# A mean over rows on one core: the first two megabytes in eight loads of sixteen partitions, and another way to fill the selector

## The chip, the cores and the metric

The kernel runs on one core of one Trainium2 chip. The metric is the device time of one execution in microseconds (us). Before the change the median of three runs is 1243.44 us (1243.44 to 1243.58).

## The reference, cut to what matters

```python
def setup_inputs():
    return {"x": np.random.randn(64, 256, 8192).astype(np.float32)}

def reference(x):
    return np.mean(x, axis=2)
```

16384 rows of 8192 float32 numbers are averaged, each to one number: 536.87 MB are read and 65.5 KB written, with about one addition for every four bytes read.

## The kernel before, in words

**Who owns which rows.** A row is 32 KB. SBUF has 128 partitions, and each partition p owns 127 rows that lie side by side in memory (`owned`, line 39), so that what partition p reads begins 127 rows, some 4.16 MB, behind what partition p-1 reads. That leaves the last 128 rows. They are cut into quarters, and each quarter row is summed in a partition of its own (`groups`, line 40).

**The loads.** There are three buffers of 128 x 16384 numbers, 8 MB each (line 53), each for a pair of rows per partition. SyncE (SP) issues every load, in one queue, in the order in which the code has them (lines 109 to 137):

- Line 114 loads the first FIRST = 2048 columns of the first pair, 1 MB over all 128 partitions, and tells `first_sem`. Line 115 loads the other 14336 columns, 7 MB, and tells `in_sems[0]`.
- Line 117 loads the second and third pair, 8 MB each.
- The loop of lines 118 to 123 waits until a buffer is free and loads the next pair into it, 60 times.
- Lines 125 to 131 load the 127th row of every partition (4 MB), three groups of quarter rows (1 MB each) and the fourth group in four pieces (448, 288, 160 and 128 KB).
- Lines 133 and 135 store the results.

**The sums.** VectorE (DVE) waits for `first_sem` (line 156). It then enters a loop that, for each buffer, waits for `in_sems[b]` and sums both rows of the pair in one reduction (line 163, 60 times), which sets the buffer free. The first reduction thus needs `first_sem` and `in_sems[0]`. The last three pairs, the single row and the quarter groups follow in straight line (lines 169 to 198), two pieces of the last group on ScalarE (ACT, lines 203 to 209).

**The selector.** A quarter group leaves one partial sum per partition, in a column of `part`; partitions 4g to 4g+3 belong to the same row g of the group. TensorE (PE) adds the four by a product with `sel`, a 128 x 32 tile that is 1/8192 where partition p belongs to row g, that is where p - 4g is 0, 1, 2 or 3, and zero elsewhere (line 218). GpSimd (POOL) makes this tile at the very start: a fill with 1/8192 (line 81) and two affine selections that put zeros on either side of the band (lines 83 and 93). PE waits for it at line 215 before anything else. POOL's next work is the scaling of the owned sums at line 104, which waits for the end.

Of the kernel before, what the change touches and what calls it, by code (L numbers as in the profile page):

```python
# [11 lines left out]
def bass_global_avg_pool_1d_kernel(  # L12
# [4 lines left out]
    P = 128  # L17
    ALIGN = 4096
    B, C, L = x.shape
    rows = B * C  # L20
    inv = 1.0 / float(L)
# [7 lines left out]
    PER = 4  # L29
    G = P // PER  # L30
# [1 line left out]
    cuts = [0, 7 * W // 16, 23 * W // 32, 7 * W // 8, W]  # L32
    pieces = [(cuts[i], cuts[i + 1]) for i in range(len(cuts) - 1)]
    NP = len(pieces)
    FIRST = L // 4

    flat = x.rearrange("b c l -> (b c) l")
    out_flat = out.rearrange("b c -> (b c)")
    owned = flat[0 : P * OWN, :].rearrange("(p r) l -> p (r l)", p=P)
# [4 lines left out]
    with ExitStack() as ctx:  # L44
# [6 lines left out]
        sel = sb("sel", [P, G])  # L51
        sb("pad", [P, (-nc.sbuf_base % ALIGN) // 4])
        bufs = [sb(f"buf{i}", [P, 2 * L]) for i in range(NBUF)]
# [6 lines left out]
        first_sem = sem("first_sem")  # L60
# [6 lines left out]
        sel_sem = sem("sel_sem")  # L67
# [10 lines left out]


        eng = nc.gpsimd  # L80
        eng.memset(sel[:], inv).then_inc(sel_sem, 1)  # L81
        eng.wait_ge(sel_sem, 1)
        eng.affine_select(  # L83
            out=sel[:],
            in_=sel[:],
            compare_op=mybir.AluOpType.is_ge,
            fill=0.0,
            base=0,
            pattern=[[-PER, G]],
            channel_multiplier=1,  # L90
        ).then_inc(sel_sem, 1)
        eng.wait_ge(sel_sem, 2)
        eng.affine_select(  # L93
            out=sel[:],
            in_=sel[:],
            compare_op=mybir.AluOpType.is_ge,
            fill=0.0,
            base=PER - 1,
            pattern=[[PER, G]],
            channel_multiplier=-1,  # L100
        ).then_inc(sel_sem, 1)
        eng.wait_ge(free_sems[0], 1)
        eng.wait_ge(owned_sem, 4)
        eng.tensor_scalar(  # L104
# [4 lines left out]
        eng = nc.sync  # L109
# [1 line left out]
        later = owned[:, 2 * NBUF * L : 2 * NB * L].rearrange(  # L111
            "p (i b w) -> b p i w", i=ROUNDS, b=NBUF
        )
        eng.dma_start(bufs[0][:, 0:FIRST], owned[:, 0:FIRST]).then_inc(first_sem, 16)
        eng.dma_start(bufs[0][:, FIRST:], owned[:, FIRST : 2 * L]).then_inc(in_sems[0], 16)
        for b in range(1, NBUF):
            eng.dma_start(bufs[b][:], pair(b)).then_inc(in_sems[b], 16)
# [23 lines left out]
        eng = nc.vector  # L141
# [11 lines left out]
                accum_out=to,  # L153
            ).then_inc(done, 1)

        eng.wait_ge(first_sem, 16)
        early = res[:, 0 : 2 * ROUNDS * NBUF].rearrange(
            "p (i b j) -> p i b j", i=ROUNDS, b=NBUF
        )
# [43 lines left out]
        eng = nc.scalar  # L203
# [8 lines left out]


        eng = nc.tensor
        eng.wait_ge(sel_sem, 3)

        def gather(dst, n, start, stop):
            return eng.matmul(dst, part[:, n : n + 1], sel[:], start=start, stop=stop)  # L218
# [41 lines left out]
```

## Time and profile before

| | |
|---|---|
| median of three runs | 1243.44 us |
| the profiled execution: its own time | 1243.53 us |
| its span, first to last instruction | 1242.3 us |
| around the span | 1.23 us |
| DVE busy | 1085.5 us, 87% of the span |
| DMA queue, packets' time | 99.8% of 16 engines' span |
| read from memory | 536.87 MB, 432 GB/s over the span |
| POOL busy, all of it | 2.1 us |
| the granted clock | 1.00 |

The span is the time from the first to the last instruction on the core. "Busy" counts an engine's own work, without its waits. The 16 DMA engines move data between memory (HBM) and SBUF in packets; a share of 99.8% says that all sixteen had a packet in hand for nearly the whole span. "SPq" and "DVEq" are the sequencers of these engines: waits, branches and the issuing of DMAs. "To landing" is the time from the issue of a DMA until its last completion.

### The profile page before, as it was taken

Reading aid. Unit: us, or ns where it says so; the run is one execution under the profiler, and the core shown is the slowest. Engines: PE = TensorE matmul, PEld = TensorE weight load, DVE = VectorE, ACT = ScalarE, POOL = GpSimd, SP = SyncE. Lnnn points to the kernel's source line nnn. Section 1 sums busy time; section 2 is a strip of 40 time slices with the busy share of each in tenths; the row PEclk is TensorE's granted clock in tenths of the full one; section 3 lists DMA queues with packets and bytes.
Section 4 is the critical chain, followed back from the end, with each engine's and each line's share of the span. In section 5 each row is a group of like instructions: output and inputs, shape, how many; then the busy total and the mean of one; then the engine's idle time right before and its main releaser. Section 6 shows DMA issues by size and latency. Waiting matters only on the chain. (4 is left out here: it accounts for less than half of the span.)

```text
span 1242.3 us, 636 instructions
## 1 busy us (share of the span) xinstructions
PE 1.7 (0%) x14; PEld 0.6 (0%) x14; DVE 1085.5 (87%) x78; ACT 3.0 (0%) x6; POOL 2.1 (0%) x8
## 2 busy tenths in 40 slices
PE   0000000000000000000000000000000000000000
PEld 0000000000000000000000000000000000000000
DVE  2898988989889898898898988989889898898988
ACT  0000000000000000000000000000000000000000
POOL 0000000000000000000000000000000000000000
DMA  9999999999999999999999999999999999999998
GB/s 405 439 439 439 439 433 411 439 439 439 439 439 422 422 439 439 439 439 439 433 411 439 439 439 439 439 437 407 439 439 439 439 439 437 409 437 439 439 439 374
DMA packets 10514, 536.94 MB, mean 432 GB/s; under 512 B 1297, under 2 KB 1554, under 8 KB 1810
## 3 DMA queue, kind: packets, MB, share of 16 engines
q1 hardware_dynamic: 10514, 536.94, 99.8%
HBM read 536.87 MB, written 0.07 MB: 432 GB/s over the span
## 5 line engine op out<-in xcount | busy, mean ns | idle before, releaser
L163 DVE TENSOR_REDUCE res<-buf 128x16384 f32 x60 | 1033.2, 17220 | 146.8 <-DVEq L162 146.8
L173 DVE TENSOR_REDUCE res<-buf 128x2 f32<-128x16384 f32 x2 | 34.4, 17220 | 4.0 <-DMA buf<-in_x_dram 4.0
L145 DVE CUSTOM_DVE_ANT_0 buf<-buf 128x4096 f32<-128x4096 f32 (+2 forms) x7 | 17.3, 2497 | 4.1 <-DMA buf<-in_x_dram 4.1
L209 ACT ACTIVATE buf<-buf 128x896 f32<-128x896 f32 (+1 forms) x2 | 1.4, 711 | 1236.7 <-DMA buf<-in_x_dram 1236.6
L104 POOL TENSOR_SCALAR scaled<-res 128x127 f32<-128x127 f32 x1 | 1.4, 1362 | 1233.3 <-DVE res L145 1233.3
L218 PE MATMUL psum<-sel,part 128*1 128x32 f32 x14 | 1.7, 225 | 1239.2 <-DVE part L145 1238.3
L209 ACT ACT_TABLE_LOAD x1 | 1.3, 1283 | 0.8 <-PEq L245 0.8
L218 PEld LDWEIGHTS psum<-sel,part 128*1 128x1 f32 x14 | 0.6, 81 | 1240.1 <-issue 1235.9
L196 DVE TENSOR_REDUCE part<-buf 128x1 f32<-128x256 f32 x1 | 0.4, 420 | 0.4 <-DMA buf<-in_x_dram 0.4
L200 DVE COPY row<-psum 1x32 f32<-1x32 f32 x1 | 0.2, 179 | 0.4 <-PE psum L218 0.4
L209 ACT ACTIVATION_READ_ACCUMULATOR buf<-buf 128x1 f32 x2 | 0.4, 188 | 0.0
L145 DVE DVE_READ_ACCUMULATOR2_ANT part<- 128x1 f32 x4 | 0.3, 82 | 0.0
L145 DVE DVE_READ_ACCUMULATOR2_ANT res<- 128x1 f32 x3 | 0.2, 83 | 0.0
L211 ACT ACTIVATE row<-psum 1x96 f32<-1x96 f32 x1 | 0.2, 223 | 0.0
L93 POOL TENSOR_SCALAR_AFFINE_SELECT sel<-sel 128x32 f32<-128x32 f32 x1 | 0.2, 215 | 0.1
L83 POOL TENSOR_SCALAR_AFFINE_SELECT sel<-sel 128x32 f32<-128x32 f32 x1 | 0.2, 213 | 0.1
L81 POOL MEMSET sel<- 128x32 f32 x1 | 0.1, 125 | 0.3 <-POOLq L245 0.3
L245 POOL MEMSET const-uint8-127<- 128x1 uint8 x1 | 0.1, 103 | 0.0
L245 POOL MEMSET const-bfloat16-1.0<- 128x1 bf16 x1 | 0.1, 102 | 0.0
L245 POOL MEMSET const-float32-0.0<- 128x1 f32 x1 | 0.1, 99 | 0.3 <-issue 0.3
L245 POOL MEMSET const-float32-1.0<- 128x1 f32 x1 | 0.1, 99 | 0.0
## 6 DMA issues: line engine op xcount, KB each, us to landing
buf<-in_x_dram SPq DMA_DIRECT2D x1, 7168.0 KB, 21.1
buf<-in_x_dram SPq DMA_DIRECT2D x4, 1024.0 KB, 34.1
buf<-in_x_dram SPq DMA_DIRECT2D x1, 4096.0 KB, 31.1
buf<-in_x_dram SPq DMA_DIRECT2D x62, 40.3
buf<-in_x_dram SPq DMA_DIRECT2D x1, 448.0 KB, 37.7
buf<-in_x_dram SPq DMA_DIRECT2D x1, 288.0 KB, 37.9
buf<-in_x_dram SPq DMA_DIRECT2D x1, 160.0 KB, 37.9
buf<-in_x_dram SPq DMA_DIRECT2D x1, 128.0 KB, 37.8
```

The costliest lines, as they stand in the source:

```text
L83: eng.affine_select(out=sel[:], in_=sel[:], compare_op=mybir.AluOpType.is_ge, fill=0.0, base=0, pattern=[[-PER, G]], channel_multiplier=1, ...
L93: eng.affine_select(out=sel[:], in_=sel[:], compare_op=mybir.AluOpType.is_ge, fill=0.0, base=PER - 1, pattern=[[PER, G]], channel_multipli ...
L104: eng.tensor_scalar(scaled[:], res[:], inv, None, op0=mybir.AluOpType.mult).then_inc(pool_sem, 1)
L145: eng.tensor_tensor_reduce(ap[:, 0:n], ap[:, 0:n], ap[:, n : 2 * n], scale=1.0, scalar=0.0, op0=ADD, op1=ADD, accum_out=to,).then_inc(done, 1)
L163: eng.tensor_reduce(early[:, bass.ds(i, 1), b, :], bufs[b][:].rearrange("p (j l) -> p j l", j=2), X, ADD,).then_inc(free_sems[b], 1)
L173: eng.tensor_reduce(res[:, 2 * g : 2 * g + 2], bufs[b][:].rearrange("p (j l) -> p j l", j=2), X, ADD,).then_inc(free_sems[0] if b == 0 els ...
L196: eng.tensor_reduce(part[:, PER + 2 : PER + 3], group(PER - 1)[:, a:z], X, ADD).then_inc(part_d, 1)
L200: eng.tensor_copy(row[:, P - G : P], psum[1][:, 0:G]).then_inc(row_sem, 1)
L209: eng.activation(ap, ap, COPY, accum_out=part[:, to : to + 1]).then_inc(part_a, 1)
L211: eng.activation(row[:, 0 : P - G], psum[0][:, 0 : P - G], COPY).then_inc(row_sem, 1)
L218: return eng.matmul(dst, part[:, n : n + 1], sel[:], start=start, stop=stop)
L245: nc = _bacc.Bacc("TRN2", target_bir_lowering=False, num_devices=1)
```

## The change

FIRST becomes 4096 columns. These first columns of the first pair, 2 MB, come in STEP = 8 loads in place of one: load j fetches 16 KB into each of the sixteen partitions j, j+8, ..., j+120, so that it has sixteen runs of 16 KB, 256 KB in all. The load behind them has the other 12288 columns, 6 MB in place of 7. DVE waits for 128 counts of `first_sem` in place of 16. The bytes that are read stay the same.

The selector is first filled with zeros, and then four affine selections, q = 0 to 3, write 1/8192 wherever p - 4g = q. Each waits for the one before it. PE waits for five counts in place of three.

```diff
-    FIRST = L // 4
+
+    FIRST = L // 2
+    STEP = 8
...
-        eng.memset(sel[:], inv).then_inc(sel_sem, 1)
-        eng.wait_ge(sel_sem, 1)
-        eng.affine_select(
-            out=sel[:],
-            in_=sel[:],
-            compare_op=mybir.AluOpType.is_ge,
-            fill=0.0,
-            base=0,
-            pattern=[[-PER, G]],
-            channel_multiplier=1,
-        ).then_inc(sel_sem, 1)
-        eng.wait_ge(sel_sem, 2)
...
+        eng.memset(sel[:], 0.0).then_inc(sel_sem, 1)
+        for q in range(PER):
+            eng.wait_ge(sel_sem, q + 1)
+            eng.affine_select(
+                out=sel[:],
+                in_=sel[:],
+                compare_op=mybir.AluOpType.not_equal,
+                fill=inv,
+                base=-q,
+                pattern=[[-PER, G]],
+                channel_multiplier=1,
+            ).then_inc(sel_sem, 1)
...
-        eng.dma_start(bufs[0][:, 0:FIRST], owned[:, 0:FIRST]).then_inc(first_sem, 16)
+        for j in range(STEP):
+            eng.dma_start(
+                bufs[0][j:P:STEP, 0:FIRST], owned[j:P:STEP, 0:FIRST]
+            ).then_inc(first_sem, 16)
...
-        eng.wait_ge(first_sem, 16)
+        eng.wait_ge(first_sem, 16 * STEP)
...
-        eng.wait_ge(sel_sem, 3)
+        eng.wait_ge(sel_sem, PER + 1)
```

More of the change, by code (lines that the diff above doesn't have):

```diff
@@ L80, in bass_global_avg_pool_1d_kernel @@
         eng = nc.gpsimd
-        eng.memset(sel[:], inv).then_inc(sel_sem, 1)
-        eng.wait_ge(sel_sem, 1)
-        eng.affine_select(
-            out=sel[:],
-            in_=sel[:],
-            compare_op=mybir.AluOpType.is_ge,
-            fill=0.0,
-            base=0,
-            pattern=[[-PER, G]],
-            channel_multiplier=1,
-        ).then_inc(sel_sem, 1)
-        eng.wait_ge(sel_sem, 2)
[L93 to L101, printed above, removed]
+        eng.memset(sel[:], 0.0).then_inc(sel_sem, 1)
[10 more added lines that the diff above has]
+            ).then_inc(sel_sem, 1)
         eng.wait_ge(free_sems[0], 1)
```

## The prediction

> **What bounds the kernel now.** I read the page first: the sliced rows, the memory line and the chain, then the loop's line.
>
> ```profile
> span 1242.3 us, 636 instructions
> ...
> DVE  2898988989889898898898988989889898898988
> ...
> DMA  9999999999999999999999999999999999999998
> ...
> HBM read 536.87 MB, written 0.07 MB: 432 GB/s over the span
> ...
> L163 DVE TENSOR_REDUCE res<-buf 128x16384 f32 x60 | 1033.2, 17220 | 146.8 <-DVEq L162 146.8
> ```
>
> The DMA row is full from the first slice to the last, DVE's is not: its 60 reductions take 17.22 us each, and 146.8 us of waiting stand before them, released by line 162, the wait for a load. So the loads are late and DVE is not. Next, busy time in stretches of time (columns: stretch, its length, then each engine, and at the end the granted clock, the DMA share and GB/s):
>
> ```profile
> 0.00:2.00 2.00, 0.00 (x0) 0.00 (x0) 0.00 (x0) 1.21 (x1) 0.74 (x7) 1.00 0.21 37
> 2.00:3.00 1.00, 0.00 (x0) 0.00 (x0) 0.00 (x0) 0.07 (x1) 0.00 (x0) 1.00 0.75 229
> 3.00:4.00 1.00, 0.00 (x0) 0.00 (x0) 0.00 (x0) 0.00 (x0) 0.00 (x0) 1.00 0.96 401
> ...
> 22.65:42.00 19.35, 0.00 (x0) 0.00 (x0) 17.24 (x2) 0.00 (x0) 0.00 (x0) 1.00 1.00 434
> ```
>
> The loads come up slowly (37, 229, 401 GB/s) and then hold 434 GB/s. Last, the start and the end in order of time:
>
> ```profile
> 0.80 0.42 SPq L114 DMA_DIRECT2D buf<-in_x_dram  x1
> 0.99 0.21 POOL L83 TENSOR_SCALAR_AFFINE_SELECT sel<-sel 128x32 f32<-128x32 f32 x1
> 1.27 0.41 SPq L115 DMA_DIRECT2D buf<-in_x_dram  x1
> 1.27 0.21 POOL L93 TENSOR_SCALAR_AFFINE_SELECT sel<-sel 128x32 f32<-128x32 f32 x1
> 1.73 1.04 SPq L117 DMA_DIRECT2D buf<-in_x_dram  x2
> 22.65 17.22 DVE L163 TENSOR_REDUCE res<-buf 128x16384 f32 x1 [22.65 <-DVEq L162]
> 40.15 19.62 SPq L121 DMA_DIRECT2D buf<-in_x_dram  x2
> ```
> ```profile
> 1239.35 0.46 DVE L145 CUSTOM_DVE_ANT_0 buf<-buf 128x288 f32<-128x288 f32 x1 [0.54 <-DMA buf<-in_x_dram]
> ...
> 1240.17 0.42 DVE L196 TENSOR_REDUCE part<-buf 128x1 f32<-128x256 f32 x1 [0.35 <-DMA buf<-in_x_dram]
> ```
>
> These add up to the span. The first packet starts at 1.8 us (the DMA view of the first 6 us is empty up to there). 536.87 MB at 434 GB/s are 1237.0 us. The last reduction starts as its load lands, at 1240.17, and 2.1 us of small work follow. 1242.3 - 2.1 - 1237.0 - 1.8 leaves 1.4 us for the slow start and the last landing. What the loads lose anywhere is lost at the end, for no later stretch has a faster rate to win it back with; what DVE, POOL or SP lose under their cover is free.
>
> **The selector.** It takes out two selections of 0.21 us and adds four of the same shape; starts lie 0.28 apart (0.99, 1.27). Four end at about 0.99 + 3 x 0.28 + 0.21 = 2.0 us, some 0.6 later than now. PE's first product comes at 1235.9 us, and POOL's next work waits for the end of the owned sums at 1234.8. That cover is 1230 us deep: 0. Without it the price would be 0.6 us.
>
> **SP's queue.** Seven more issues stand ahead of line 115's. One takes 0.42 us, and starts lie 0.47 apart (0.80, 1.27, 1.73), so 7 x 0.47 = 3.3 us: line 115 is issued at about 4.6, line 117 by 5.5. SP's next task is at 40.15. The DMA engines must not run dry meanwhile. A 256 KB load at 434 GB/s lasts 0.60 us, longer than the 0.47 of an issue, and the eight last 4.8, from 1.8 to 6.6 or later, while line 115's packets can start at 4.6 + 1.0 = 5.6 (the first load: issued at 0.80, first packet 1.8). Cover of 1.0 us: 0. If an issue took 0.65 us, it would be gone.
>
> **More completions.** Seven more loads must each report. At the tail, 288 KB land between ACT's start at 1238.67 and DVE's at 1239.35, 0.68 us, just what 434 GB/s makes of them; the next 160 and 128 KB take 0.82 instead of 0.68, so 0 to 0.07 us a load, 0 to 0.5 for seven. I take 0.2.
>
> [...]
>
> **DVE's first wait** for 128 counts ends well before line 115's load lands, which DVE awaits next: 0.
>
> **Sixteen partitions at a time.** Here is the price that decides. Every load of this trace that carries weight covers all 128 partitions, and sixteen DMA engines together hold 434 GB/s, 27.1 each. Where that ceiling sits, no row tells. If each engine has it by itself, eight loads cost nothing more. [...] 2.097 MB at 434 GB/s are 4.83 us, at 217 they are 9.66. The ends are 0 and +4.83 (coarser groupings, four engines to an entry, would give +14.5). [...] That is a judgement; the trace holds no transfer over fewer partitions at a rate that tells.
>
> [...]
>
> **Sum.** 1243.53 (the profiled execution) + 4.83 + 0.2 - 0.3 = 1248.26. The profiled execution stands 0.09 above the median: 1248.2 us. Own range of this case: 1247.1 (the whole start won) to 1248.8.
>
> **Rivals.**
>
> 1. *Full rate, not slower.* Place: the eight loads. If each DMA engine carries its ceiling with it, or entries serve eight neighbours, 2 MB still take 4.83 us. Then only start and completions count: 1243.44 - 0.3 + 0.2 = 1243.3, between 1242.0 and 1243.9. [...] For it: loads of 8 MB and of 288 KB get the same 434, as an engine-bound ceiling would have it. Against it: nothing in the trace shows sixteen scattered partitions at that rate. 0.25.
>
> [...]
>
> [...]
>
> 4. *It does not do what it says*, or worse sharing: loads of sixteen runs on fewer engines, or four engines to an entry: +14.5 and more, 1258 and up. 0.05.
>
> **Chances.** A measurement of this kernel can tell about 0.2% from no change, 2.5 us. Two to an entry in step: 0.50, slower. Rival 2: 0.05 slower, 0.05 same. Rival 1: 0.24 same, 0.01 faster (the start cannot give more than 1.4 us, so this is for what I have not seen). Rival 3: same. Rival 4: slower. Slower 0.60, same 0.39, faster 0.01. The range from 1243.0 to 1249.0 leaves out rival 4 and the faster third of rival 1, some 0.13.
>
> **What the trace after would show.** Sharing: the first 10 us at about 217 GB/s, packets of the first loads at double length, DVE's first reduction near 27.4 us in place of 22.65, all later steps shifted by as much, the stretch behind still at 434. Full rate: first reduction at 22.4 to 22.8. [...] Selector: four selections over by 2.1 us and PE's first product still released by DVE. Issues: line 115's at 4.6. The forecast fails if the first reduction starts before 26, or if a later stretch is above 434 GB/s and wins the loss back.

## The result, and the profile after

The changed kernel takes 1248.00 us (median of seven runs, 1247.93 to 1248.06), the kernel before 1243.49 (1243.44 to 1243.69): 4.51 us more, a ratio of 1.0036 with a 95% interval of 1.0026 to 1.0045. 1248.2 was forecast. The profiled execution took 1247.93 us.

The page of the changed kernel:

```profile
span 1246.6 us, 648 instructions
...
DVE  1988989889898898898988989889889898898988
...
DMA  9999999999999999999999999999999999999998
...
HBM read 536.87 MB, written 0.07 MB: 431 GB/s over the span
...
L159 DVE TENSOR_REDUCE res<-buf 128x16384 f32 x60 | 1033.2, 17220 | 151.2 <-DVEq L158 151.2
```

DVE's work is the same to a tenth of a microsecond, its waiting for loads is 4.4 us longer (146.8 before). The DMA row is as full as before, which misleads: an engine counts as busy while its packet is under way, however slowly it moves (a share of 1.01 at 216 GB/s and of 1.00 at 433 below). What tells is the rate beside the share. Busy time by stretches, with the DMA share and GB/s in the last two columns:

```profile
2.00:4.00 2.00, 0.00 (x0) 0.00 (x0) 0.00 (x0) 0.01 (x1) 0.23 (x2) 1.00 1.07 270
4.00:10.00 6.00, 0.00 (x0) 0.00 (x0) 0.00 (x0) 0.00 (x0) 0.00 (x0) 1.00 1.01 216
27.00:46.36 19.36, 0.00 (x0) 0.00 (x0) 17.22 (x1) 0.00 (x0) 0.00 (x0) 1.00 1.00 433
```

In a short stretch the share can stand over 1 (before, from 4 to 5 us, it is 2.15 with 918 GB/s), so a packet seems to be booked whole in one stretch; GB/s divided by the share is the rate of sixteen busy engines. From 4 to 10 us it is 216/1.01 = 214 GB/s, half of the 433 of a later stretch. The engines were not starved, their packets were slow.

The start and the end of the changed kernel in order of time:

```profile
0.72 0.12 POOL L83 MEMSET sel<- 128x32 f32 x1 [0.29 <-POOLq L241]
0.72 5.01 SPq L108 DMA_DIRECT2D buf<-in_x_dram  x8
1.09 1.28 POOL L86 TENSOR_SCALAR_AFFINE_SELECT sel<-sel 128x32 f32<-128x32 f32 x4 [0.24 <-POOL sel L83]
5.78 0.59 SPq L111 DMA_DIRECT2D buf<-in_x_dram  x1
6.41 0.90 SPq L113 DMA_DIRECT2D buf<-in_x_dram  x2
27.46 17.22 DVE L159 TENSOR_REDUCE res<-buf 128x16384 f32 x1 [27.46 <-DVEq L158]
44.95 19.58 SPq L117 DMA_DIRECT2D buf<-in_x_dram  x2
```
```profile
1240.34 0.27 PE L214 MATMUL psum<-sel,part 128*1 128x32 f32 x2 [1240.34 <-DVE part L141]
```

The time from issue to landing says the same without the shares. In the changed kernel it grows from 3.6 us for the first of the eight loads to 7.7 for the last (least, median and longest):

```profile
DMA to landing us min/median/max: 3.6/5.7/7.7
```

That is 0.59 us more from load to load. Issued 0.63 us apart, the loads landed 1.22 apart, and 0.262 MB in 1.22 us are 215 GB/s.

The first reduction starts at 27.46 in place of 22.65, 4.81 us later; all that follows keeps this distance but for 0.4 us. The four selections are over by 2.4 us, and PE's first product is released by DVE as before.

### The profile page after: what moved, and what is told of

The parts are those of the page before. It is cut to its first block, busy times and chain, and to the rows that moved or that the text cites. A ratio compares the mean times of both kernels' runs of the same rounds, so it can differ in the third digit from the quotient of the medians.

```text
span 1246.6 us, 648 instructions
## 1 busy us (share of the span) xinstructions
PE 1.7 (0%) x14; PEld 0.6 (0%) x14; DVE 1085.5 (87%) x78; ACT 3.0 (0%) x6; POOL 2.5 (0%) x10
```

## The experiments

Line numbers differ a little from kernel to kernel. Losses are differences of the medians against the kernel before, which stood between 1243.46 and 1243.53 us beside every group of runs. Three theories compete. **One**: two DMA engines meet at one entry of SBUF, because a load touches only sixteen partitions. **Two**: memory is slow at sixteen rows 33 MB apart. **Three**: eight loads, with their issues and completions, starve the engines. An "entry" is the author's word for a way into SBUF that several partitions would share. It is an assumption, and no row of a profile names one; what the runs can show is whether the rate goes with the partitions that are written.

### e1: the loads without the selector

The selector is that of before, the loads are those of the change.

> The eight loads of the change with the selector of before. Whatever makes the loads slow, the selector lies under 1230 us of cover: 1248.0 us, as with both parts (between 1247.8 and 1248.2). If the selector had a part in it, the time would lie between 1243.5 and 1247.5.

Measured: 1248.08 us (1248.01 to 1248.17), ratio 1.0037 [1.0022, 1.0051]. The loss is the loads' alone.

### e8: one load of the same size

```diff
-        for j in range(STEP):
-            eng.dma_start(
-                bufs[0][j:P:STEP, 0:FIRST], owned[j:P:STEP, 0:FIRST]
-            ).then_inc(first_sem, 16)
+        eng.dma_start(bufs[0][:, 0:FIRST], owned[:, 0:FIRST]).then_inc(first_sem, 16)
...
-        eng.wait_ge(first_sem, 16 * STEP)
+        eng.wait_ge(first_sem, 16)
```

> The first 4096 columns in one load over all 128 partitions, with the selector of the change: neither the size of the first part nor the selector is left as a cause. All theories: 1243.5 us (1243.2 to 1243.8), first reduction at 22.65.

Measured: 1243.50 us (1243.38 to 1244.15), ratio 1.0000 [0.999, 1.0009], first reduction at 22.57. Neither the new selector nor the 2 MB matter; it is the way the loads are cut.

### e2: eight loads cut by columns

```diff
         for j in range(STEP):
-            eng.dma_start(
-                bufs[0][j:P:STEP, 0:FIRST], owned[j:P:STEP, 0:FIRST]
-            ).then_inc(first_sem, 16)
+            a, z = j * FIRST // STEP, (j + 1) * FIRST // STEP
+            eng.dma_start(bufs[0][:, a:z], owned[:, a:z]).then_inc(first_sem, 16)
```

> Eight loads of 256 KB as in the change, with as many issues and completions, but each over all 128 partitions and 512 columns (2 KB a run). Theory one, two DMA engines meet at one entry of SBUF because a load touches only sixteen partitions: the 4.5 us go, and what stays is the price of shorter runs and seven completions, 0 to 0.8 us: 1243.5 to 1244.3 us, first reduction at 22.6 to 23.4. Theory two, memory: sixteen runs in rows 33 MB apart are slow to read; here every load reads from all 128 rows, as before: also 1243.5 to 1244.3. Theory three, eight issues and eight completions in a row starve the DMA engines: 1248.0 as in the change.

Measured: 1245.14 us (1244.67 to 1245.46), ratio 1.0013 [1.0003, 1.0022], first reduction at 24.83. The loss is 1.6 us, twice the upper end that theory one allowed, and far from the 4.5 of theory three. Eight loads have a price of their own, here with runs of 2 KB. Their busy engines move 293/0.94 = 312 GB/s:

```profile
4.00:8.00 4.00, 0.00 (x0) 0.00 (x0) 0.00 (x0) 0.00 (x0) 0.00 (x0) 1.00 0.94 293
```

### e3 and e4: the destination or the source

e3 keeps the partitions and changes the rows; e4 keeps the rows and changes the partitions.

```diff
-                bufs[0][j:P:STEP, 0:FIRST], owned[j:P:STEP, 0:FIRST]
+                bufs[0][j:P:STEP, 0:FIRST], owned[16 * j : 16 * (j + 1), 0:FIRST]
```
```diff
-                bufs[0][j:P:STEP, 0:FIRST], owned[j:P:STEP, 0:FIRST]
+                bufs[0][16 * j : 16 * (j + 1), 0:FIRST], owned[j:P:STEP, 0:FIRST]
```

> Load j writes the same sixteen partitions as in the change, eight apart, but reads the rows of partitions 16j to 16j+15, 4.16 MB apart instead of 33 MB. The first 4096 columns thus land in other partitions than they belong to, and the sums of these rows are others; bytes, runs and loads are the same. Theory one (entries of SBUF): the destination decides, 1248.0 us, first reduction at 27.4, the loads at half of 434 GB/s for 10 us. Theory two (memory): the time moves off 1248.0, to 1243.5 if rows 33 MB apart were the cause, or to something longer if near rows are worse.

> The mirror image: load j reads the rows of the change, 33 MB apart, but writes the sixteen neighbours 16j to 16j+15. The first 4096 columns land in other partitions than they belong to, and the sums of these rows are others. [...] Theory two (memory): the reads are those of the change, so 1248.0. [...]

Measured: e3 1248.02 us (1248.00 to 1248.48), ratio 1.0037 [1.0023, 1.0052]; e4 1254.50 us (1254.30 to 1254.86), ratio 1.0088 [1.0072, 1.0105]. Busy time by stretches, first of e3, then of e4:

```profile
4.00:10.00 6.00, 0.00 (x0) 0.00 (x0) 0.00 (x0) 0.00 (x0) 0.00 (x0) 1.00 0.98 210
```
```profile
4.00:10.00 6.00, 0.00 (x0) 0.00 (x0) 0.00 (x0) 0.00 (x0) 0.00 (x0) 1.00 1.04 128
```

With other rows the rate stays at 210/0.98 = 214 GB/s; with other partitions it falls to 128/1.04 = 123. The destination decides, and theory two is out. It is not the number of partitions in a load either: the change and e4 both write sixteen at a time. Rival 4 of the prediction named a loss of 14.5 us, that of a quarter of the rate (108 GB/s); e4, with 123 GB/s and a loss of 11.0 us, stays short of that.

### e5: seven apart

```diff
         for j in range(STEP):
-            eng.dma_start(
-                bufs[0][j:P:STEP, 0:FIRST], owned[j:P:STEP, 0:FIRST]
-            ).then_inc(first_sem, 16)
+            s = slice(j, 112, 7) if j < 7 else slice(112, 128)
+            eng.dma_start(bufs[0][s, 0:FIRST], owned[s, 0:FIRST]).then_inc(first_sem, 16)
```

> Seven loads of sixteen partitions seven apart (j, j+7, ... for j = 0 to 6, partitions 0 to 111), and an eighth of the sixteen neighbours 112 to 127; same bytes, loads and run length as the change. [...] Theory two (memory): rows 29 MB apart instead of 33, no reason for another time than 1248.0.

Measured: 1248.01 us (1247.46 to 1248.36), ratio 1.0035 [1.0021, 1.0049], first reduction at 27.54. The time is the 1248.0 of theory two, which e3 and e4 have put out; the rates are not those of the change:

```profile
2.00:4.00 2.00, 0.00 (x0) 0.00 (x0) 0.00 (x0) 0.01 (x1) 0.22 (x2) 1.00 1.04 320
4.00:8.00 4.00, 0.00 (x0) 0.00 (x0) 0.00 (x0) 0.00 (x0) 0.00 (x0) 1.00 0.89 283
8.00:12.00 4.00, 0.00 (x0) 0.00 (x0) 0.00 (x0) 0.00 (x0) 0.00 (x0) 1.00 1.17 266
```

From 4 to 8 us the loads run at 283/0.89 = 318 GB/s in place of 214, with sixteen partitions per load as in the change: other partitions, another rate. The gain is lost again at the end. Issue by issue, the first six loads land 0.84 us apart, the sixth at 8.5 us (10.5 in the change). The seventh lands at 10.7 and the eighth, the sixteen neighbours, at 13.1 (12.9 in the change): the last two together take 4.6 us. Against 0.60 us a load at 434 GB/s, the last two lose 3.4, the intervals before them 1.2, and the first packets come 0.3 later; that is the 4.9 us by which the first reduction is late. Why the seventh is held up as well was not separated.

### e6 and e11: 32 and 64 partitions at a time

```diff
-    STEP = 8
+    STEP = 4
```
```diff
-    STEP = 8
+    STEP = 2
```

> STEP = 4: four loads of 32 partitions, four apart, 16 KB runs, 512 KB each. [...] Theory three (number of loads): half of the loss, 1245.7.

> STEP = 2: two loads of 64 partitions, two apart, 1 MB each. [...]

Measured: four loads 1244.69 us (1244.53 to 1244.97), ratio 1.0010 [1.0000, 1.0019]; two loads 1243.86 us (1243.71 to 1244.07), ratio 1.0003 [0.9993, 1.0012], which is no difference that can be told. Stretches of e6, then of e11:

```profile
4.00:8.00 4.00, 0.00 (x0) 0.00 (x0) 0.00 (x0) 0.00 (x0) 0.00 (x0) 1.00 0.98 360
```
```profile
4.00:8.00 4.00, 0.00 (x0) 0.00 (x0) 0.00 (x0) 0.00 (x0) 0.00 (x0) 1.00 1.26 541
```

360/0.98 = 367 and 541/1.26 = 429 GB/s. A load need not cover all 128 partitions to get the full rate: 64 two apart do. Half as many loads lose 1.2 us, where theory three had half of the loss, 2.2. Why 32 and 64 partitions are not held at half rate was not shown: which engine gets which run is not in these views.

### e7: twice the bytes

```diff
-    FIRST = L // 2
+    FIRST = L
```

> FIRST = 8192: eight loads of sixteen partitions eight apart with runs of 32 KB, 4 MB in all. Theory one: twice the bytes at half rate, twice the loss of 4.83: 1243.5 + 9.66 - 0.3 = 1252.9 us (1252.3 to 1253.3), first reduction near 32.3. Theory three (issues and completions, the same eight): 1248.0, or less, since the longer loads cover the issues better.

Measured: 1253.64 us (1253.62 to 1253.76), ratio 1.0081 [1.0065, 1.0098]. As many loads, twice the bytes, and 10.1 us lost in place of 4.5. From 4 to 10 us the busy engines move 262/1.28 = 205 GB/s:

```profile
4.00:10.00 6.00, 0.00 (x0) 0.00 (x0) 0.00 (x0) 0.00 (x0) 0.00 (x0) 1.00 1.28 262
```

The loss goes with the bytes at half rate, not with the number of loads. It is 0.7 us more than forecast; that the rate is a little under half goes that way.

### e9 and e10: another order, other partitions

```diff
-        for j in range(STEP):
+        for j in (0, 4, 1, 5, 2, 6, 3, 7):
```
```diff
         for j in range(STEP):
-            eng.dma_start(
-                bufs[0][j:P:STEP, 0:FIRST], owned[j:P:STEP, 0:FIRST]
-            ).then_inc(first_sem, 16)
+            k = 32 * (j // 2) + j % 2
+            s = slice(k, k + 32 - j % 2, 2)
+            eng.dma_start(bufs[0][s, 0:FIRST], owned[s, 0:FIRST]).then_inc(first_sem, 16)
```

> The eight loads of the change in the order j = 0, 4, 1, 5, 2, 6, 3, 7; nothing else. [...] Any theory of memory or of the number of loads: 1248.0.

> Eight loads of sixteen partitions two apart (16 of 32 neighbours at a time). [...]

Measured: e9 1246.99 us (1246.84 to 1247.53), ratio 1.0029 [1.0018, 1.0039]; e10 1248.13 us (1248.00 to 1248.44), ratio 1.0038 [1.0023, 1.0052]. Stretches of e9, then of e10:

```profile
4.00:10.00 6.00, 0.00 (x0) 0.00 (x0) 0.00 (x0) 0.00 (x0) 0.00 (x0) 1.00 1.05 251
```
```profile
4.00:10.00 6.00, 0.00 (x0) 0.00 (x0) 0.00 (x0) 0.00 (x0) 0.00 (x0) 1.00 1.04 219
```

The mere order of the same eight loads moves the time by 1.0 us, and its runs do not overlap with those of the change; no theory of memory or of numbers has that. But the rate rises from 214 to 251/1.05 = 239 GB/s only, and why the order counts can't be told from these. e10 loses what the change does, at 219/1.04 = 211 GB/s: sixteen partitions two apart, within 32 neighbours, go at the rate of sixteen eight apart (214).

### e12: eight loads of 64 partitions

Eight loads of 256 KB once more, each of 64 partitions two apart and 1024 columns, in runs of 4 KB.

```diff
         for j in range(STEP):
+            k, a = j % 2, j // 2 * FIRST // 4
             eng.dma_start(
-                bufs[0][j:P:STEP, 0:FIRST], owned[j:P:STEP, 0:FIRST]
+                bufs[0][k:P:2, a : a + FIRST // 4], owned[k:P:2, a : a + FIRST // 4]
             ).then_inc(first_sem, 16)
```

> [...] Theory one: 1243.9 to 1245.1 us (from the two loads' 0.4 to the 1.65 of eight loads with 2 KB runs), with 350 to 434 GB/s from 4 to 8 us; the sharing is then 2.9 to 4.1 of the 4.5 us. If eight stepped loads in a row were slow by themselves: 1248.0.

Measured: 1246.06 us (1245.56 to 1246.36), ratio 1.0020 [1.0010, 1.0029]. That lies between the two expectations ("sharing" is theory one's word for what the half rate costs). Stretches:

```profile
2.00:4.00 2.00, 0.00 (x0) 0.00 (x0) 0.00 (x0) 0.00 (x1) 0.22 (x2) 1.00 0.90 293
4.00:8.00 4.00, 0.00 (x0) 0.00 (x0) 0.00 (x0) 0.00 (x0) 0.00 (x0) 1.00 0.93 288
```

Here the share is under 1 and the rate 288/0.93 = 310 GB/s, without any halving. Late issues are not the cause. At 288 GB/s a load takes 0.91 us, longer than the 0.63 between two issues, and the time to landing grows from 2.9 us for the first load to 5.1 for the last:

```profile
DMA to landing us min/median/max: 2.9/4.0/5.1
```

So the loads queue up, and what is slow is small loads back to back, by whatever mechanism. The rates of e2 (312) and of e5's first loads (318) are nearly the same. In one, two, four and eight loads that are not held at half rate (e8 at 524/1.22 = 430 GB/s from 4 to 8 us, e11 at 429, e6 at 367, e12 at 310), the 2 MB lose 0.0, 0.4, 1.2 and 2.6 us. From two loads on that is 0.3 to 0.4 for each further one, and e2, whose destination is not stepped, loses 0.2 for each of seven; the 0.4 of two can be mostly the later first packets of a stepped destination (see "Size" below). The run length was not held the same: 16 KB in e11 and e6, 4 KB in e12.

Eight stepped loads of 256 KB thus cost up to 2.6 us even without the half rate. Taken as a difference, the half rate is at least 1.9 of the change's 4.5 us, and at most 4.1 (against the two loads of e11, which lose 0.4). But the two prices need not add: at half rate the engines were always busy (share 1.01), the loads landed 1.2 us apart as 214 GB/s have it, and twice the bytes in as many loads lost 10.1 us (e7). That fits a price per load that is hidden behind the slower packets; no run shows it directly.

## Why the prediction was right, point by point

- **The bound.** The loads set the end, and what they lose stays lost: confirmed but for 0.4 us. The first reduction is 4.81 us late, the sum of DVE's waits only 4.4:

```profile
DVE res L163 <- DVEq L162: 146.8, 60, 22.7
```
```profile
DVE res L159 <- DVEq L158: 151.2, 60, 27.5
```

 The first line is of before, the second of after; the numbers are the total, the count and the longest wait, which is the first. The other 59 are 124.1 and 123.7. So 0.4 us came back in later pairs, against the forecast that nothing would. Why the rate there is a few hundredths of a per cent better was not tried.

- **Sixteen partitions at a time**, +4.83, the term that decided. It is shown that the loads go at half rate with the engines busy (214 GB/s at a share of 1.01), and that the partitions they write set the rate: deaf to the source (e3, 214), moved by the destination (e4, 123) and by the order (e9, 239), growing with the bytes (e7, 10.1 us lost), and but for the price of a load gone with other partitions (e6, 367, and e11, 429). The term itself, 2.097 MB at half of 434 GB/s, was the author's estimate: that engines meet at entries of SBUF is shown by no run, and what the runs show in its place is a rate that goes with the partitions written. It was a judgement between 0 and 4.83, since the trace before could not decide it.

- **Size.** 4.7 forecast, 4.51 measured. The smaller terms were less good than the sum. The 0.3 taken off for the start is shown by no run; the first packets lost about that instead: the DMA view has them at 2.1 us after an issue at 0.72, where before it was 1.8 after 0.80, 1.4 us instead of 1.0. It goes with the stepped destination, not with the number of runs: e4, with sixteen runs into neighbours, has its first packets 1.0 us after the issue, and e11, with 64 runs two apart, has none before 2 us, 1.27 after it. Nor does the main term fit to the tenth: 2.097 MB at 214 GB/s are 9.80 us, 4.97 more than at 434. With the later first packets that would make 5.27, and the first reduction is 4.81 late. About 0.5 us was won, then; before, the third and fourth microsecond ran at 229 and 401 GB/s, some 0.55 us short of 434, and this the halved loads may hide (an estimate, not tested). With the 0.4 us that came back later, errors of both signs cancel: that the total came within 0.2 us is in part luck.

- **SP's queue.** An issue takes 0.59 us and not 0.42, and starts lie 5.06/8 = 0.63 apart, so line 115's load is issued at 5.78 and not at 4.6. I had given 0.65 as the point where the cover is gone. It was no price here because the eight loads were landing until 12.9 us; in e12, with the same issues, the loads also queue up, so there it was none either. By the same numbers it would be one only for loads that take less than 0.63 us each (an estimate).

- **More completions**, 0.2: not to be seen by themselves, but e2 (1.6) and e12 (2.6) say that eight loads in a row cost more than that when nothing slower hides it. So rival 1 was priced wrongly: at full rate the change would have come to 1243.3 by my sum, while e12, eight loads without the half rate, takes 1246.06, with runs of a quarter of the length.

- **The selector**: 0, as said. Four selections, over by 2.4 us and not 2.0; e8 carries them and takes 1243.50.

- **Rivals.** A first reduction at 27.46, 4.81 us late, with a share of 1.01 at half rate, leaves no room for idle engines or for half of the loss alone, and so none for rivals 2 and 3. Rival 4 asked for 14.5 us and more.

## What to carry to other kernels

Read the DMA share and the GB/s of a stretch together: full share at half the rate (here 1.01 at 216 GB/s) says that packets are slow, and the next question, which decided here, is which partitions they go to. When a load is cut, keep many partitions, spread over SBUF, in every piece (here two loads of 64 partitions two apart cost nothing that could be told, four of 32 four apart 1.2 us, eight of sixteen eight apart 4.5, eight of sixteen neighbours 11.0), and keep the pieces few, for small loads in a row had a price even without the half rate (here 0.2 to 0.4 us for each further load of 256 or 512 KB). In a kernel that moves memory at its ceiling from the first microsecond to the last, a loss at the start is a loss at the end (here 4.81 us at the first reduction, 4.51 in the whole time).

## What the runs showed of the hardware that was not expected

- The issue of a load whose destination steps over partitions takes 0.57 to 0.59 us in the median, whatever the step (the change and 7 apart 0.589, 4 apart 0.580, 2 apart 0.570); into sixteen neighbours, with a stepped source, it takes 0.42:

```profile
L108 SPq DMA_DIRECT2D buf<-in_x_dram x8: 569/589/592, 0.7 to 5.1; - x8
```
```profile
L108 SPq DMA_DIRECT2D buf<-in_x_dram x8: 403/420/420, 0.7 to 3.9; - x8
```

 The first line is the issue line of the changed kernel, the second that of e4 (least, median and longest duration in ns). The load issued just behind the stepped ones (line 111 after) takes 0.59 as well, although it steps over nothing. In e5 the eighth load, into neighbours, still takes 0.59 behind seven stepped ones, and the load behind it 0.41.

- The slow rates are no round parts of 434 GB/s: sixteen neighbours went at 123 (e4; a quarter is 108), sixteen eight apart at 214 (the change; half is 217), and the same eight loads in another order at 239 (e9). Why is not in these views.
